# Layer 1's joined attention weights: eight of ten key chunks turned by the transposing DMA instead of four, with a new order of work

## The chip, the cores and the metric

One NeuronCore of one Trainium2 chip runs the whole program. The metric is device time in microseconds (us) of that core, median over runs. The kernel before takes 1679.44 us (three runs, 1678.99 to 1679.91).

## The reference, cut to what matters

Two layers over 1024 latent tokens and 256 context tokens, width 1024. Layer 0 is multi-head latent attention; the change leaves its instructions as they are. Layer 1 is differential attention with 8 heads: each head has two queries and two keys of 64 channels and one value of 128 channels.

```
scale = B_HEAD ** -0.5
o1 = attention(q[..., 0], k[..., 0], v)      # over 1024 latent keys + 256 context keys
o2 = attention(q[..., 1], k[..., 1], v)
o = o1 - lam_full * o2                        # the two maps share v
o = rms_norm(o, g_sub) * (1.0 - lambda_init)
o = o * silu(gate)
x = layer_norm(ALPHA * x + gate * (o @ out_w), ln_g, ln_b)
```

Since both maps multiply the same v, the kernel joins the two softmax maps into one weight matrix, p0 - lam * p1, before the product with v. Only the latent tokens are wanted after layer 1, so there are 8 heads x 8 tiles of 128 queries: 64 units, each over 1280 keys (10 chunks of 128).

## The kernel before

**One unit of layer 1** (`attend`, L1786 on). PE makes five PSUM banks of scores (L1845, L1846). DVE takes maxima (L1863 over the context, L1867 over the latent keys) and bounds (L1869); ACT takes exponentials into SBUF (L1874). DVE sums and joins: L1882 to L1884, then L1887, one instruction over 128x1280 in fp32, here called the **join**. The joined weights stand with queries on partitions; the product with v needs keys on partitions, so each 128x128 chunk has to be turned, and it is wanted in two float16 parts (high and low).

There are two ways to turn a chunk, and `KD` (L77) says how many chunks take which:

- *The PE way* (`turns`): PE transposes chunks KD to 9 in fp32 into PSUM (L1788; four chunks, then two), ACT writes the high part `ph` (L1793) and DVE the low part `pl` (L1795), both from PSUM.
- *The DMA way* (`far`): ACT writes the high part of chunks 0 to KD-1 into `dd` (L1892, **far.hi**), DVE the low part (L1893, **far.lo**), both from SBUF, and one transposing DMA on SP's queue turns both into `pd` (L1895, **far.move**). `dd` has one buffer, `pd` two.

`values` then makes 30 products of 128 columns into one PSUM bank (L1810 to L1812, **pv**), first those from `ph` and `pl`, then those from `pd`; ACT scales the result (L1816) and squares it (L1817), POOL normalises it and it goes to DRAM.

**What else PE does meanwhile.** While head h is attended, PE makes the keys, queries and values of head h+1 (`mm3`, L217 to L219); these fill the time in which a unit waits for other engines. During head 7 there is no next head; instead the output projection of finished tiles (`out_tile`, turns L1953, products L217 to L219 in fp32) fills it. It can begin only after the value buffers of the last head are let go: ACT's L1738 and POOL's L1739 split the values, ACT's L1741 makes the gate, SP stores it (L1742) and loads whole rows of it back (L1939), POOL multiplies (L1940), and PE turns (L1953).

**What sets the order.** `heads1` writes every piece of work of layer 1 with an engine, a cost and a due time into a list (`Plan.add`). `Plan.run` takes pieces from it by start time and, among those that could start within `EPS1` of the earliest on their engine, by due time; each kind's due time is moved by the table `OFF`, and nothing more than `AHEAD` ahead of the rest is taken. The resulting order is the program: every engine works through its own list in order, so a wait at its head holds all that stands behind. The table, `EPS1` and `AHEAD` are numbers written in the kernel; no part of the order is decided on the chip.

## Time and profile before

| | us |
|---|---|
| median of 3 runs | 1679.44 |
| profiled execution, its own time | 1678.12 |
| its span in the trace | 1676.3 |
| layer 0 and projections, up to the first unit | about 915 |
| heads 0 to 6 of layer 1, with the next head's projections | about 597 |
| head 7, with the output projection | about 164 |

A profile gives, for each engine, when it was busy. Each engine works in order, so an idle stretch ahead of an instruction means that it waited; the trace names the instruction whose end released it. A PE that is busy 98% of a stretch is what the stretch lasts by, and work of other engines there costs nothing until it makes PE wait. PE's matmuls overlap: the time that one occupies PE is the distance from its start to the next one's start, not its own duration.

### The profile page before, as it was taken

To read this page: it belongs to the slowest core of one execution; us is meant where nothing else is said; L and a number is where in the kernel's file an instruction comes from. 1 tells how busy PE (TensorE), PEld (TensorE's weight loads), DVE (VectorE), ACT (ScalarE), POOL (GpSimd) and SP (SyncE) were. 2 spreads that over 40 slices of the span, in tenths; PEclk is the share of its full clock that TensorE was granted. 3 is DMA by queue.
4 is the path that set the end of the run, shared out by engine and by line. 5 is a ranking of instruction groups with operands and counts; after the bars stand their busy time and mean duration, and the time that the engine had idled before them with its cause. 6 is when DMAs were issued, how large, how long until landed. Compare 5 with 4: busy or idle time off the path is not lost.

```text
span 1676.3 us, 36592 instructions
## 1 busy us (share of the span) xinstructions
...
## 2 busy tenths in 40 slices
...
GB/s 319 91 132 232 206 81 21 42 33 42 39 36 42 39 52 45 104 167 204 177 113 79 72 101 102 102 102 105 98 95 86 96 84 92 59 156 89 146 135 76
DMA packets 183932, 171.63 MB, mean 102 GB/s; under 512 B 82024, under 2 KB 159432, under 8 KB 183759
## 3 DMA queue, kind: packets, MB, share of 16 engines
...
## 4 chain that ended last, share of the span: by engine, by line
PE 65%; DVE 19%; ACT 9%; issue 3%; DMA 2%; POOL 2%; POOLq 0%; DVEq 0%; SPq 0%; ACTq 0%
PE ps_s L217 5%; PE ps_s L219 5%; PE ps_s L218 5%; PE ps_a L969 4%; PE ps_a L970 4%; PE ps_a L971 4%; PE ps_a L217 3%; PE ps_a L219 3%; PE ps_a L218 3%; ACT p L1874 3%; PE ps_a L920 3%; DVE mx L1867 3%; DVE p L1887 3%; PE ps_d L994 2%; PE ps_d L987 2%
## 5 line engine op out<-in xcount | busy, mean ns | idle before, releaser
L979 POOL TENSOR_TENSOR pl<-p,ph 128x1024 f16<-128x1024 f32 (+1 forms) x176 | 370.2, 2117 | 102.7 <-ACT ph L977 68.6
L975 ACT ACTIVATE p<-ps_a,esc 128x1024 f32<-128x1024 f32 (+1 forms) x176 | 188.7, 1072 | 58.9 <-PE ps_a L971 52.4
L924 DVE TENSOR_REDUCE mx<-ps_a 128x1 f32<-128x1024 f32 x128 | 156.2, 1222 | 72.1 <-PE ps_a L920 71.5
L1874 ACT ACTIVATE p<-ps_p,mx 128x512 f32<-128x512 f32 x256 | 175.5, 689 | 31.4 <-DVE mx L1869 30.6
L977 ACT CAST ph<-p 128x1024 f16<-128x1024 f32 (+1 forms) x176 | 177.0, 1006 | 7.0 <-PE ps_d L988 1.8
L1867 DVE TENSOR_REDUCE mx<-ps_p 128x1 f32<-128x512 f32 x256 | 164.2, 680 | 1.9 <-PE ps_p L1846 1.9
L969 PE MATMUL ps_a<-qH,KH 100*128 100x512 f16 x320 | 122.0, 381 | 3.1 <-DVE mx L924 2.3
L970 PE MATMUL ps_a<-qH,KL 96*128 96x512 f16 x320 | 121.5, 380 | 0.0
L971 PE MATMUL ps_a<-qL,KH 96*128 96x512 f16 x320 | 120.7, 377 | 0.0
L1795 DVE SCALAR_TENSOR_TENSOR pl<-ps_t,lcf,ph 128x512 f16<-128x512 f32 (+1 forms) x128 | 78.2, 611 | 42.5 <-ACT ph L1793 41.9
L1887 DVE SCALAR_TENSOR_TENSOR p<-p,sm,p 128x1280 f32<-128x1280 f32 x64 | 106.1, 1658 | 1.7
L1845 PE MATMUL ps_p<-KS,QS 128*128 128x512 f16 x256 | 98.1, 383 | 9.5 <-ACT p L1874 9.5
L987 PE MATMUL ps_d<-Vh,ph 128*128 128x65 f16 x1344 | 103.7, 194 | 2.0 <-ACT ph L977 1.7
L988 PE MATMUL ps_d<-Vl,ph 128*128 128x64 f16 x1344 | 103.2, 194 | 0.0
L1793 ACT ACTIVATE ph<-ps_t,lcf 128x512 f16<-128x512 f32 (+1 forms) x128 | 74.8, 584 | 39.3 <-PE ps_t L1788 38.1
L1846 PE MATMUL ps_p<-KS,Q 128*128 128x512 f16 x256 | 98.2, 383 | 0.0
L987 PEld LDWEIGHTS <-ph 128*128 128x128 f16 x1344 | 89.0, 98 | 11.2 <-issue 4.8
L988 PEld LDWEIGHTS <-ph 128*128 128x128 f16 x1344 | 87.3, 98 | 3.8
L191 POOL TENSOR_SCALAR ss<-ss 128x1 f32<-128x1 f32 x64 | 20.4, 318 | 119.1 <-ACT ps_t L1817 117.4
L920 PE MATMUL ps_a<-KH,qH 96*128 96x512 f16 x256 | 76.1, 379 | 0.0
L936 DVE TENSOR_REDUCE mx<-ps_a 128x4 f32<-128x1024 f32 (+1 forms) x48 | 50.3, 1048 | 33.9 <-PE ps_a L931 33.9
L1810 PE MATMUL ps_t<-vh,ph 128*128 128x128 f16 x384 | 68.4, 221 | 6.4 <-DVE pl L1795 6.3
...
## 6 DMA issues: line engine op xcount, KB each, us to landing
ws<-in_dw SPq DMA_DIRECT2D x28, 512.0 KB, 3.9
adw<-in_ada_w SPq DMA_DIRECT2D x24, 512.0 KB, 4.5
adaw<-in_ada_w SPq DMA_DIRECT2D x16, 512.0 KB, 6.8
g<-sg_d SPq DMA_DIRECT2D x16, 512.0 KB, 3.5
...
```

What stands on the lines that cost most here:

```text
L924: add("m.max", "D", 1.223, lambda t=t, ps=ps: dve.tensor_reduce(mx.tile[:, t, 0:1], ps.tile, axis=AX.X, op=ALU.max), r=[ps], w=[(mx, t)] i ...
L969: pe.matmul(s_, KH[i][:nr, ks], QH.tile[:nr, :], start=True, stop=False)
L970: pe.matmul(s_, KL[i][:DQ, ks], QH.tile[:DQ, :], start=False, stop=False)
L971: pe.matmul(s_, KH[i][:DQ, ks], QLo.tile[:DQ, :], start=False, stop=True)
L975: add("s.exp", "A", 1.114 if x else 0.682, lambda st=st, p32=p32: act.activation(p32.tile[:, :2 * n], st.tile[:, :2 * n], AF.Exp, scale=esc0),
L977: add("s.hi", "A", 1.046 if x else 0.618, lambda p32=p32, ph=ph: act.copy(ph.tile[:, :2 * n], p32.tile[:, :2 * n]), r=[p32], new=[ph], hol ...
L979: add("s.lo", "G", 2.14 if x else 1.17, lambda p32=p32, ph=ph, pl=pl: pool.tensor_tensor(pl.tile[:, :2 * n], p32.tile[:, :2 * n], ph.tile[ ...
L987: pe.matmul(v_()[:, t, :], w, Vh[:, k, h, :], start=(k == kcs[0] and t == 0), stop=False, skip_group_check=True)
L988: pe.matmul(v_()[:, t, :V0], w, Vl[:, k, h, :], start=False, stop=False, skip_group_check=True)
L1867: add(f"max{m}", "D", 0.68, lambda i=i, b_=b_: dve.tensor_reduce(mx.tile[:, 2 + 2 * m + i:3 + 2 * m + i], b_.tile, axis=AX.X, op=ALU.max, ...
L1874: add(f"exp{m}", "A", 0.78 if n == 512 else 0.57, lambda i=i, c0=c0, n=n, b=b, lo=lo: act.activation(p[m].tile[:, c0:c0 + n], b.tile[:, lo ...
L1887: add("join", "D", 1.65, lambda: dve.scalar_tensor_tensor(p[0].tile, p[1].tile, sm.tile[:, 4:5], p[0].tile, op0=ALU.mult, op1=ALU.add), r= ...
```

## The change

`KD` goes from 4 to 8. Per unit, PE turns two chunks (one group) where it turned six (two groups); far.hi and far.lo work on 1024 columns where they worked on 512; the transposing DMA turns 16 blocks of 128x128 (512 KB) where it turned 8 (256 KB). `pv` now starts with two chunks from `ph` and `pl` and takes eight from `pd`.

The buffers follow: `dd` and each `pd` double, `ph` and `pl` shrink to a third, `o1` goes from three buffers to two, a few constants of layer 0 (`onr`, `adac`, `cct`, `cols0`) move into a pool that closes with layer 0's first part, and `gb3` (the broadcast `ln_b`) moves to a pool that opens later, so its load now waits for `OPEN` rather than `PRJ`. The table `OFF`, `EPS1` and `AHEAD` are new, so layer 1's whole list is in another order.

```diff
-EPS1 = dict(P=0.05, A=0.05, D=0.2, G=0.2)
-AHEAD = 3.75
+EPS1 = dict(P=0.05, A=0.05, D=0.15, G=0)
+AHEAD = 3.5
-OFF = {"bound0": -5.35, "bound1": -0.75, "exp0": -1.25, "exp1": -2.1, "far.hi": -6.65, "far.lo": -2.1, "far.move":
+OFF = {"bound0": -7.75, "bound1": -2.7, "exp0": -0.85, "exp1": -2.0, "far.hi": -5.9, "far.lo": -1.95, "far.move":
...
-KD = 4
+KD = 8
...
-    onr = col(P, "onr", F32R)
-    adac = col(16, "adac")
-    cct = col(16, "cct")
+    p0 = ctx.enter_context(ExitStack())
+    early_ = p0.enter_context(spool("early"))
+    onr = early_.tile([P, P], F32R, name="onr")
+    adac = early_.tile([P, 16], F32, name="adac")
+    cct = early_.tile([P, 16], F32, name="cct")
...
-            "o1": ([P, P], F32, 3), "mx": ([P, 8], F32, 2), "sm": ([P, 8], F32, 4),
+            "o1": ([P, P], F32, 2), "mx": ([P, 8], F32, 2), "sm": ([P, 8], F32, 4),
...
-                for k0, n, a in ((0, 4, PR["t0"]), (4, 2, PR["t1"])):
+                for k0, n, a in ((0, 2, PR["t0"]),):
...
-                add("far.hi", "A", 0.72, lambda: act.activation(dd.tile[:, 0, :], p[0].tile[:, :KD * P], AF.Copy, scale=lcf[:, 0:1]), r=[p[0]], new=[dd], hold=0.63, at=g + PR["fa"])
+                add("far.hi", "A", 1.24, lambda: act.activation(dd.tile[:, 0, :], p[0].tile[:, :KD * P], AF.Copy, scale=lcf[:, 0:1]), r=[p[0]], new=[dd], hold=1.15, at=g + PR["fa"])
...
-            TAG1["g"] = ([P, D], F32, 2)
+            TAG1["g"], TAG1["gb3"], place["gb3"] = ([P, D], F32, 2), ([P, D], F32, 1), place["g"]
...
-                add("o.gb", "S", 4.0, lambda: bcast_row(GB[1].tile, ln_b[1:2, :]), r=[PRJ], new=[GB[1]], hold=0.06, at=g + 6.5)
...
+        add("o.gb", "S", 4.0, lambda: bcast_row(GB[1].tile, ln_b[1:2, :]), r=[OPEN], new=[GB[1]], hold=0.06, at=g)
```

(The planner's costs of far.lo and far.move change in the same way as far.hi's. Lines of the changed kernel stand one higher than before in layer 1: L1893 is L1894 there.)

Where the new order matters, three places. First, DVE's list in head 5, tile 4, from the join on. `mx` are the maxima, `dd` is far.lo, `pl` the PE way's low part, `wx` and `wy` the next head's weights. Before:

```order
L1863 TENSOR_REDUCE mx_20044<-ps_c_19994 128x2
L1867 TENSOR_REDUCE mx_20044<-ps_p_19937 128x1
L1867 TENSOR_REDUCE mx_20044<-ps_p_19952 128x1
L1869 TENSOR_SCALAR mx_20044<-mx_20044 128x1
L1893 SCALAR_TENSOR_TENSOR dd_20053<-p_3048_19919,lcf,dd_20053 128x512
L1867 TENSOR_REDUCE mx_20044<-ps_p_19969 128x1
L1867 TENSOR_REDUCE mx_20044<-ps_p_19988 128x1
L1869 TENSOR_SCALAR mx_20044<-mx_20044 128x1
L1795 SCALAR_TENSOR_TENSOR pl_20128<-ps_t_20091,lcf,ph_20100 128x512
L1613 SCALAR_TENSOR_TENSOR wx_20002<-ws_19513,uw_19800,wx_20002 128x1024
L1613 SCALAR_TENSOR_TENSOR wy_20022<-ws_19514,uw_19800,wy_20022 128x1024
L1795 SCALAR_TENSOR_TENSOR pl_20128<-ps_t_20145,lcf,ph_20100 128x256
```

The same place now:

```order
L1864 TENSOR_REDUCE mx_19710<-ps_c_19671 128x2
L1868 TENSOR_REDUCE mx_19710<-ps_p_19584 128x1
L1868 TENSOR_REDUCE mx_19710<-ps_p_19605 128x1
L1870 TENSOR_SCALAR mx_19710<-mx_19710 128x1
L1894 SCALAR_TENSOR_TENSOR dd_19715<-p_2994_19575,lcf,dd_19715 128x1024
L1868 TENSOR_REDUCE mx_19710<-ps_p_19682 128x1
L1868 TENSOR_REDUCE mx_19710<-ps_p_19687 128x1
L1870 TENSOR_SCALAR mx_19710<-mx_19710 128x1
L1796 SCALAR_TENSOR_TENSOR pl_19793<-ps_t_19707,lcf,ph_19729 128x256
L1614 SCALAR_TENSOR_TENSOR wx_19685<-ws_19347,uw_19611,wx_19685 128x1024
L1614 SCALAR_TENSOR_TENSOR wy_19739<-ws_19348,uw_19611,wy_19739 128x1024
```

far.lo stands where it stood, behind three maxima, but is twice as wide; of the two low parts of the PE way, the 512-wide one is gone.

Second, ACT's list at the end of head 6, where the last head's values are finished: L1738 (now L1739) splits the values, L1741 (now L1742) makes the gate, L1892 (now L1893) is far.hi. Before, from far.hi of head 6's last tile on; the gate (L1741) and the last two copies of values stand directly ahead of it:

```order
L1892 ACTIVATE dd_21813<-p_3321_21698,lcf 128x512
L1816 ACTIVATE o_3335_21817<-ps_t_21760,sm_21541 128x128
L1874 ACT_TABLE_LOAD
L1874 ACTIVATE p_3336_21820,sm_21821<-ps_p_21753,mx_21803 128x512
L1817 ACTIVATE ps_t_21760,ss_21824<-o_3335_21817 128x128
L1874 ACTIVATE p_3336_21820,sm_21821<-ps_p_21799,mx_21803 128x512
L1874 ACTIVATE p_3342_21841,sm_21821<-ps_p_21805,mx_21803 128x512
L1793 ACTIVATE ph_21846<-ps_t_21836,lcf 128x512
L1874 ACTIVATE p_3342_21841,sm_21821<-ps_p_21808,mx_21803 128x512
L1874 ACTIVATE p_3342_21841,sm_21821<-ps_c_21794,mx_21803 128x256
L1874 ACTIVATE p_3336_21820,sm_21821<-ps_c_21794,mx_21803 128x256
L1738 CAST vh_21863<-Vf_21301 128x1280
```

Now, up to far.hi of the same tile:

```order
L1736 COPY gg_20822<-ps_s_21176 128x256
L1734 ACTIVATE Vf_20875<-ps_s_21176,kc_95 128x256
L1875 ACTIVATE p_3264_21324,sm_21290<-ps_p_21248,mx_21256 128x512
L1739 CAST vh_21333<-Vf_20875 128x1280
L1875 ACTIVATE p_3264_21324,sm_21290<-ps_p_21253,mx_21256 128x512
L1875 ACTIVATE p_3264_21324,sm_21290<-ps_c_21228,mx_21256 128x256
L1817 ACTIVATE o_3270_21369<-ps_t_21326,sm_20975 128x128
L1742 ACT_TABLE_LOAD
L1742 ACTIVATE gg_20822<-gg_20822,uw_20212 128x1024
L1818 ACTIVATE ps_t_21326,ss_21388<-o_3270_21369 128x128
L1893 ACTIVATE dd_21391<-p_3257_21289,lcf 128x1024
```

The split of the values stood behind far.hi of head 6's last tile and a whole unit's exponentials; it now stands one exponential behind the last copy of values, ahead of that far.hi.

Third, SP's queue at the same place. `pd<-dd` is far.move; the first of each listing is that of head 6's tile 7 (before) and tile 6 (now). `sg_d<-gg` stores the gate, `g<-sg_d` loads it back, `wsq` and `gb` are the broadcast rows. Before:

```order
L1895 DMA_TRANSPOSE pd_21826<-dd_21813 128x8x128
L1831 DMA o_d_100<-o_3335_21817 128x128
L1895 DMA_TRANSPOSE pd_21925<-dd_21879 128x8x128
L1742 DMA sg_d_98<-gg_21274 128x8x128
L1165 DMA wsq_21965<-in_ln_g 128x1024
L1939 DMA g_21967<-sg_d_98 128x1024
L1831 DMA o_d_100<-o_3355_21918 128x128
L1939 DMA g_21994<-sg_d_98 128x1024
L1895 DMA_TRANSPOSE pd_22054<-dd_22031 128x8x128
```

Now:

```order
L1896 DMA_TRANSPOSE pd_21307<-dd_21261 128x16x128
L1939 DMA ws_21312<-o_d_103 128x896
L1939 DMA ws_21380<-o_d_103 128x896
L1743 DMA sg_d_101<-gg_20822 128x8x128
L1939 DMA ws_21401<-o_d_103 128x896
L1940 DMA g_21421<-sg_d_101 128x1024
L1166 DMA gb_3285_21423<-in_ln_b 128x1024
L1166 DMA wsq_21425<-in_ln_g 128x1024
L1832 DMA o_d_103<-o_3270_21369 128x128
L1896 DMA_TRANSPOSE pd_21431<-dd_21391 128x16x128
```

The gate's store and its first load stood behind far.move of head 7's first tile; they now stand ahead of far.move of head 6's last tile, two transposing DMAs earlier. In PE's list the scores of about 2.3 units stand between the last product of the values and the first turn of the output projection before, and of about 1.4 units now. In the steady part a unit's pv stood behind the second to fifth score bank of the unit two on; now it mostly stands behind the first or second bank of the unit three on.

## Rows read from the trace of the kernel before

**Rows 1.** Busy us and instructions of each engine by stretch; granted clock, DMA share, GB/s.

```profile
1005.00:1512.00 507.00, 497.40 (x4302) 365.63 (x4300) 456.52 (x839) 411.45 (x1065) 251.21 (x308) 1.00 0.41 98
1512.00:1541.70 29.70, 17.14 (x137) 11.42 (x134) 23.99 (x36) 25.14 (x54) 13.60 (x13) 0.83 0.37 94
...
1556.00:1676.30 120.30, 112.31 (x702) 88.51 (x700) 82.05 (x144) 50.76 (x126) 67.06 (x62) 0.98 0.37 115
```

**Rows 2.** DVE's waits, 1005 to 1512 us: us in total, times, longest.

```profile
DVE pl L1795 <- ACT ph L1793: 28.1, 27, 1.7
```

**Rows 3.** PE in order of time, one group of four turns: start, us, instruction.

```profile
1207.07 0.60 PE L1788 MATMUL ps_t<-idr,p 128*128 128x128 f32 x4
...
1207.51 0.38 PE L217 MATMUL ps_s<-h1H,wy 128*128 128x512 f16 x1
```

**Rows 4.** Groups by shape, 915 to 1655 us: busy us, mean ns | idle before.

```profile
L1893 DVE SCALAR_TENSOR_TENSOR dd<-p,lcf,dd 128x512 f16<-128x512 f32 x64 | 58.1, 907 | 1.5 <-ACT dd L1892 1.3 <-issue 0.2
...
L1795 DVE SCALAR_TENSOR_TENSOR pl<-ps_t,lcf,ph 128x512 f16<-128x512 f32 x64 | 47.5, 743 | 26.0 <-ACT ph L1793 26.0
L1892 ACT ACTIVATE dd<-p,lcf 128x512 f16<-128x512 f32 x64 | 46.0, 718 | 27.0 <-DVE p L1887 20.1 <-issue 5.2 <-ACT kH L1679 0.7
...
L1793 ACT ACTIVATE ph<-ps_t,lcf 128x512 f16<-128x512 f32 x64 | 43.9, 686 | 22.6 <-PE ps_t L1788 22.5
...
L1793 ACT ACTIVATE ph<-ps_t,lcf 128x256 f16<-128x256 f32 x64 | 30.9, 483 | 16.7 <-PE ps_t L1788 15.6
L1795 DVE SCALAR_TENSOR_TENSOR pl<-ps_t,lcf,ph 128x256 f16<-128x256 f32 x63 | 30.2, 480 | 16.5 <-ACT ph L1793 15.9
...
L1613 DVE SCALAR_TENSOR_TENSOR wx<-ws,uw,wx 128x1024 f16<-128x1024 f32 x13 | 21.1, 1620 | 0.0
...
L1611 ACT ACTIVATE wx<-ws,uw 128x1024 f16<-128x1024 f32 x13 | 15.1, 1158 | 0.3
```

**Rows 5.** Two lines of DVE: ns min/median/max, first and last start.

```profile
L1795 DVE SCALAR_TENSOR_TENSOR pl<-ps_t,lcf,ph x128: 470/609/752, 931.8 to 1655.2; 128x512 f16<-128x512 f32 x64, 128x256 f16<-128x256 f32 x64
...
L1893 DVE SCALAR_TENSOR_TENSOR dd<-p,lcf,dd x64: 740/743/2918, 929.0 to 1649.4; 128x512 f16<-128x512 f32 x64
```

**Rows 6.** far.move, ns min/median/max and landing; the page's plain 512 KB load (us).

```profile
L1895 SPq DMA_TRANSPOSE pd<-dd x64: 1232/1244/2240, 929.8 to 1651.5; - x64
...
DMA to landing us min/median/max: 3.0/3.1/4.4
...
g<-sg_d SPq DMA_DIRECT2D x16, 512.0 KB, 3.5
```

**Rows 7.** One unit in order of time, DVE, ACT, SP and PE: start, us.

```profile
1202.96 2.41 DVE L1887 SCALAR_TENSOR_TENSOR p<-p,sm,p 128x1280 f32<-128x1280 f32 x1
...
1205.41 0.72 ACT L1892 ACTIVATE dd<-p,lcf 128x512 f16<-128x512 f32 x1 [0.71 <-DVE p L1887]
...
1207.39 0.74 DVE L1893 SCALAR_TENSOR_TENSOR dd<-p,lcf,dd 128x512 f16<-128x512 f32 x1
...
1208.20 1.25 SPq L1895 DMA_TRANSPOSE pd<-dd  x1
...
1213.66 1.56 DVE L1887 SCALAR_TENSOR_TENSOR p<-p,sm,p 128x1280 f32<-128x1280 f32 x1
...
1215.17 0.22 PE L1810 MATMUL ps_t<-vh,pd 128*128 128x128 f16 x1
1215.23 0.22 PE L1811 MATMUL ps_t<-vl,pd 128*128 128x128 f16 x1
```

**Rows 8.** From the last values to the first turn of the output projection, in time.

```profile
1521.45 1.29 ACT L1738 CAST vh<-Vf 128x1280 f16<-128x1280 f32 x1
...
1530.59 0.57 SPq L1742 DMA_DIRECT2D sg_d<-gg  x1
...
1534.48 0.32 SPq L1939 DMA_DIRECT2D g<-sg_d  x1
...
1541.75 0.66 PE L1953 MATMUL ps_t<-idr,ws 128*128 128x128 f32 x4 [1.82 <-POOL ws L1940]
```

More of the change, by code (lines that the diff above doesn't have):

```diff
@@ L43 @@
 PR = dict(s0=0.0, mx=0.1, ex=0.2, t0=0.15, t1=0.4, s1=0.3, pv=0.7, jo=0.6, fa=0.75)
-EPS1 = dict(P=0.05, A=0.05, D=0.2, G=0.2)
-AHEAD = 3.75
+EPS1 = dict(P=0.05, A=0.05, D=0.15, G=0)
+AHEAD = 3.5
 SP0, SP1, SP2 = 0.0, 0.3, 3.3
-OFF = {"bound0": -5.35, "bound1": -0.75, "exp0": -1.25, "exp1": -2.1, "far.hi": -6.65, "far.lo": -2.1, "far.move":
-       3.05, "g.add": 0.6, "g.bias": 2.4, "g.keep": -1.25, "g.load": 0.25, "g.sum": -0.9, "g.zero": 0.35, "join":
-       -0.35, "k.ctx": -2.6, "k.hi": 0.4, "k.lo": -4.1, "k.move": 2.95, "late": -2.2, "max.c": -0.1, "max0": -7.45,
-       "max1": 0.15, "o.ga": -3.35, "o.gb": 2.0, "o.hi": 2.4, "o.lo": -1.9, "o.load": -3.1, "o.mul": -1.8, "open":
-       -1.65, "prod": 0.2, "pv": -4.6, "pv.gate": -0.65, "pv.norm": 1.1, "pv.out": -1.2, "pv.sq": -5.9, "pv.store":
-       -6.45, "pv.us": 1.9, "q.hi": 2.05, "q.lo": 1.5, "q.move": -5.7, "r.add": -2.6, "r.cos": 1.3, "r.out": 0.1,
-       "r.sin": -7.3, "r.swap": -0.15, "score0": 0.45, "score1": 0.35, "scorec": -0.05, "sums": -3.95, "turn.hi0":
-       -3.05, "turn.hi4": -5.7, "turn.lo0": 1.05, "turn.lo4": -3.25, "turn0": -0.3, "turn4": -2.6, "v.gate": -1.6,
-       "v.hi": 1.15, "v.keep": 1.5, "v.lo": -2.05, "v.octx": -1.7, "v.out": 2.55, "v.pctx": 0.05, "v.silu": 0.95,
-       "v.store": 4.4, "v.turn": -2.5, "w.hi": -0.85, "w.lo": 0.4, "w.load": -2.65, "w.root": -3.8, "w.scale": 2.3,
-       "w.sq": 1.4, "w.sum": -3.5, "w.unit": 0.6, "w.us": -0.25, "x.gate": 1.05, "x.hi": -0.65, "x.lo": 1.15,
-       "x.load": 3.15, "x.low": 4.3, "x.mul": 5.75, "z.add": -0.9, "z.agg": 0.15, "z.bn": 0.6, "z.end": 2.7, "z.g":
[3 rows of a table removed]
@@ new lines @@
+OFF = {"bound0": -7.75, "bound1": -2.7, "exp0": -0.85, "exp1": -2.0, "far.hi": -5.9, "far.lo": -1.95, "far.move":
+       2.25, "g.add": 0.05, "g.bias": 2.25, "g.keep": -1.65, "g.load": 0.2, "g.sum": -2.2, "g.zero": -1.5, "join":
+       -0.5, "k.ctx": -1.35, "k.hi": 2.7, "k.lo": 0.55, "k.move": 3.6, "late": -2.55, "max.c": -0.1, "max0": -11.6,
+       "max1": -0.4, "o.ga": 3.35, "o.gb": 3.1, "o.hi": 2.25, "o.lo": 0.85, "o.load": -3.7, "o.mul": -0.7, "open":
+       -5.4, "prod": 0.6, "pv": -6.15, "pv.gate": -0.5, "pv.norm": 0.9, "pv.out": -3.4, "pv.sq": -9.9, "pv.store":
+       -7.3, "pv.us": 1.8, "q.hi": 2.6, "q.lo": 0.15, "q.move": -7.6, "r.add": -3.25, "r.cos": 2.05, "r.out": -1.9,
+       "r.sin": -5.6, "r.swap": 1.65, "score0": 0.45, "score1": 0.35, "scorec": -0.45, "sums": -5.05, "turn.hi0":
+       -0.9, "turn.hi4": -5.7, "turn.lo0": 2.55, "turn.lo4": -3.25, "turn0": -1.95, "turn4": -2.6, "v.gate": -1.0,
+       "v.hi": -3.15, "v.keep": 2.45, "v.lo": -5.2, "v.octx": 1.7, "v.out": 2.35, "v.pctx": -0.4, "v.silu": -1.05,
+       "v.store": -0.15, "v.turn": -1.85, "w.hi": 1.9, "w.lo": 1.25, "w.load": -0.5, "w.root": -0.8, "w.scale": 2.1,
+       "w.sq": 1.45, "w.sum": -1.2, "w.unit": 0.05, "w.us": -2.6, "x.gate": -1.0, "x.hi": -3.15, "x.lo": 2.15,
+       "x.load": -3.65, "x.low": 2.4, "x.mul": 5.15, "z.add": -3.85, "z.agg": 0.95, "z.bn": 0.6, "z.end": -2.65,
[3 rows of a table added]
@@ L161, in hybrid_kernel @@
     gsub = col(1, "gsub")
-    cols0 = cpool.tile([P, 16, 2], F32, tag="cols0", name="cols0")
+    cols0 = early_.tile([P, 16, 2], F32, name="cols0")
     cols1 = cpool.tile([P, 16, 2], F32, tag="cols1", name="cols1")
@@ L197, in hybrid_kernel @@
     latL = lat.tile([P, 3, NTOK], F32R, name="latL")
-    p0 = ctx.enter_context(ExitStack())
     hp = p0.enter_context(spool("p0"))
```

10 lines of the change are left out of this document (5 added, 5 removed), and 6 rows, old and new, of the table OFF.

## The prediction, made before the changed kernel ran

> **What bounds the kernel now.** I read the windows first. From 1005 to 1512 us (heads 1 to 6) PE is busy 497.4 of 507.0 us at a granted clock of 1.00, DVE 456.5, ACT 411.5 [rows 1]: the reader is to see that this stretch lasts as long as PE's list, with DVE close behind. Head 7 from 1556 us on is also PE's, 112.3 of 120.3. Between them lies a gap, 1512 to 1541.7, where PE has 17.1 us of work in 29.7 us and its granted clock falls to 0.83 on average, between the levels of 1.2 and 2.4 GHz [rows 1]. Then I read the waits of DVE, since it is next: of its 50.5 idle us in the long stretch, 28.1 are waits of the PE way's low part for ACT's high part [rows 2]. Last I followed one unit through DVE, ACT, SP's queue and PE [rows 7] and the gap through its links [rows 8].
>
> The sum is made against the profiled execution's own 1678.1 us (span 1676.3); that is 1.3 us under the median of the three runs, 1679.4, so 1.3 is added at the end.
>
> **PE's turns.** A group of four turns holds PE from 1207.07 to the next matmul's start at 1207.51, 0.44 us [rows 3] (the 0.60 shown includes the tail that the next one overlaps). This group goes, once in each of 64 units: 64 x 0.44 = 28.2 us of PE. pv keeps its 30 products; nothing is added on PE. Where PE is the bound all of it is gained, so the upper bound is 28.2 (1.3 of it in the three units of the gap, where PE waits anyhow; I leave it in); the lower one depends on DVE and on the DMA, next.
>
> **ACT.** Removed per unit: a 512-wide copy from PSUM (0.686) and the 512-wide far.hi (0.718) [rows 4]. Added: a 1024-wide far.hi, by the row of the same shape, L1611, 1.158. Net -0.25 us; ACT had 95 us to spare in 507, so this is worth nothing by itself.
>
> **DVE.** Removed: the 512-wide low part, 0.743, and the 512-wide far.lo, 0.907 in the mean [rows 4]. Added: a 1024-wide far.lo. Twice the step from 256 to 512 columns (0.743 - 0.480 = 0.263) on top of 0.743 gives 1.27 for it undisturbed; the wide row L1613 on `wx` has a mean of 1.62 [rows 4]. I take 1.27 plus the 0.16 by which far.lo's mean now stands over its median of 0.743 [rows 5], so 1.43. DVE saves 1.65 - 1.43 = 0.22 us per unit, bounds 0.03 and 0.38. Rows 1 hold 48 units: DVE's work falls from 456.5 to 446, PE's time from 507 to 507 - 48 x 0.44 = 485.9. That leaves DVE 40 us of idle time where it had 50.5. It has to lose 10.5 us of waiting, and a source is there: a unit had two waits of the low part, and has one now, behind two maxima and a bound in DVE's list. If half of the 28.1 us goes, 36 us of idle time are left, under the 40. So PE stays the bound, with 4 us to spare in 486. I count the whole 28.2.
>
> Which form of DVE work is left matters here. far.lo reads both operands from SBUF and ran up to 2918 ns where its median is 743; the low part of the PE way reads one from PSUM and never passed 752 in 128 instructions [rows 5]. The Trainium skill, "SBUF — State Buffer", section "Who interferes with whom", says that a DVE instruction with two SBUF inputs contends with a GpSimd instruction that reads SBUF, and that whichever starts first holds the other off; the trace agrees, with those two maxima. It speaks against this change, which moves DVE work from the form that is never held off to the one that is: by it far.lo's mean would be nearer the 1.62 of L1613, DVE's work in the long stretch 9 us more, its idle time 31 us where I want 36, and the gain there some 5 us less.
>
> By rows alone that end is the 0.03, and it is kept in the first rival.
>
> **The transposing DMA.** far.move takes 1.244 us on SP's queue and lands 3.1 us after its issue [rows 6]. Twice the blocks: between 4.35 (only the issue part doubles) and 6.2 us (all of it doubles); less than 3.1 is excluded, since nothing of the transfer is left out. I take 4.35: the nearest row of that size, a plain 512 KB load, lands in 3.5 [rows 6], by that end. Who waits for it is pv. In the unit of rows 7 the DMA is issued at 1208.20 and its result is first used at 1215.17, 6.97 us later, so 3.9 us are to spare. Used up: 0.53 by the longer far.lo (far.hi, 0.44 longer, still ends ahead of it), 1.25 to 3.1 by the DMA, and 0.7 because pv reaches `pd` after two chunks where it did after six (12 products, 0.06 us from start to start [rows 7]). That is 2.5 to 4.3 of 3.9; PE's new list puts pv about half a unit later against the scores, some 5 of the 10.7 us that a unit takes there [rows 7], which gives back more than is missing. Cost taken: nothing. SP's queue has room, and what stands behind far.move (stores of a unit's output) nobody waits for at once.
>
> **The gap.** Its links before: the last values split at 1521.45, the gate stored at 1530.6, loaded back from 1534.5, first turn at 1541.75 [rows 8]. The store stood behind two far.moves and the split behind an exponential group, not behind missing data. The new lists put the split about one unit and the store two far.moves earlier, and PE has scores of 1.4 units there for 2.3. PE's idle time in the gap is 29.7 - 17.1 = 12.6 us over three units [rows 1], 4.2 each: one unit fewer saves 4.2. Bounds: all 12.6, or one unit more, +4.2.
>
> **Costed at nothing.** The constants that move: layer 0's lists are the same, and the new pool closes where the old buffers' last readers are long done. `o1`'s third buffer: hidden by ACT's idle time, 95 us over 48 units [rows 1], some 2 us each; without that cover pv's output would wait for a store of about as long. `gb3`'s load is later by the opening of its pool, hidden by the first output tile, whose end is its first reader; uncovered it costs one 512 KB load, 3.5 [rows 6].
>
> **Sum.** 1678.1 - 28.2 - 4.2 = 1645.7 in the profiled execution; with 1.3, a median of 1647.0. Its own range: the gap's bounds (-8.4, +8.4) and PE's 9.6 us of remaining idle time in the long stretch, some of which may go: 1634 to 1657.
>
> **Rivals.** *DVE takes over.* PE's turns go, but DVE's waits are replaced by others as its list tightens, and idle time stays at 50.5. For it: DVE is busy 90% now and would be 92%; far.lo, now twice as long, stands ahead of two maxima that free score banks. Against it: half of DVE's idle time is tied to what is removed. Then a unit shortens by DVE's 0.22 alone: 64 x 0.22 = 14, gap unchanged: 1664, median 1665; with DVE's saving at its lower bound (0.03), 1676 to 1677.
>
> *pv waits for the DMA (the change doesn't do what it says).* If landing is 6.2 or more and the later place of pv is worth little, each unit waits 0.4 to 0.6 us and gives back the 0.44: 1675 to 1688. For it: the spare 3.9 above; against it: the unit is pipelined deeper.
>
> *The single `dd` buffer (slower).* far.hi of a unit must wait until the DMA of the unit before has read `dd`. The loop is far.hi to issue (1205.41 to 1208.20, 2.79 [rows 7]; 3.3 with the wider far.lo) plus landing: 7.7 to 9.5 us against a unit of 10.70 (1202.96 to 1213.66 [rows 7]). It decides once landing passes 7.4 us; at 8 us each of 56 units outside head 7 costs 0.6 more than before: +34 us, 1712. For it: one buffer, and other DMAs fill 0.41 of the engines' time; against it: the longest landing now is 4.4 [rows 6].
>
> **How the numbers follow.** Forecast 0.72; DVE takes over 0.18; pv waits 0.06; the `dd` loop 0.04. The likeliest is 1647. A range for 8 in 10 reaches from 1634 to 1668: the forecast's own, and the middle of DVE's case. A measurement of this kernel can tell 0.2%, 3.4 us, from no change. Faster: the forecast, DVE's case but for 0.01, and 0.02 of pv's, together 0.91; same: that 0.01 and 0.02 of pv's, 0.03; slower: the last 0.02 of pv's and the `dd` loop, 0.06.
>
> **What would show it.** Right: 128 turns in place of 384 and a far.move that lands in 4.3 to 5 us; heads 1 to 6 shorter by 3.5 us each at a PE busy share still near 98%; DVE's waits for ACT's high part halved; the first turn of the output projection 20 to 25 us after the last values. Wrong: a PE busy share of 95% or less in heads 1 to 6, with waits of pv for `pd` (the second rival), for maxima or joins (the first), or of ACT ahead of far.hi for a DMA (the third); or a gap as long as before.

## The result, and the profile after

The changed kernel takes 1683.25 us in the median of 16 runs (1679.68 to 1688.34), the kernel before 1679.39 in the same job: a ratio of 1.0025, with a 95% interval of 1.0017 to 1.0033. The forecast was 1647.0, with a range of 1634 to 1668; it was wrong in sign and by 36 us. The profiled execution has a span of 1682.0 us for 1676.3.

PE's turns did go: its busy time over the whole span falls from 1610.6 to 1590.1 us. The time did not follow. These are the windows of the changed kernel, in the columns of [rows 1]:

```profile
1005.00:1512.00 507.00, 479.86 (x4101) 343.79 (x4099) 453.78 (x787) 407.02 (x1012) 279.36 (x309) 1.00 0.52 118
1512.00:1541.70 29.70, 16.06 (x137) 12.16 (x135) 24.61 (x30) 22.57 (x49) 21.38 (x18) 0.83 0.71 196
1556.00:1682.00 126.00, 113.02 (x710) 88.10 (x708) 84.67 (x147) 52.77 (x134) 69.05 (x65) 0.99 0.48 131
```

In the long stretch PE's share falls from 98.1 to 94.6%: it now waits inside it. DVE does about as much as before, 453.8 us for 456.5 [rows 1]. A fixed window holds different amounts of work in the two kernels, so the same five heads are set side by side: from the join of head 1's first unit to that of head 6's. (The join of head 7's first unit would be a bad end: it stands 1 us behind the split of the last values before, and 20 us behind it now, so that the window would take in the gap in one kernel alone.) The first line is before, the second after.

```profile
1009.70:1437.90 428.20, 419.65 (x3629) 308.28 (x3628) 388.24 (x713) 352.37 (x905) 205.77 (x257) 1.00 0.40 95
```

```profile
1013.50:1444.70 431.20, 407.25 (x3479) 291.64 (x3478) 387.67 (x676) 351.27 (x869) 232.46 (x259) 1.00 0.52 118
```

Five heads last 3.0 us longer. PE is busy for 12.4 us less. DVE is busy for as long as before, and its idle time grows from 40.0 to 43.5 us. By the forecast's own terms the five heads were to last 428.2 - 40 x 0.44 = 410.6, with DVE busy for 388.2 - 40 x 0.22 = 379.4 and idle for 31.2. So of the 20.6 us that are missing here, 8.3 are DVE's work and 12.3 its waiting. Of the rest of the program, what lies ahead of these heads takes 3.8 us longer, and what lies behind them 1.1 us less.

The work. These groups of DVE, by shape, are from 1005 to 1512 us; first before, then after (busy us, mean ns, idle before it):

```profile
L1887 DVE SCALAR_TENSOR_TENSOR p<-p,sm,p 128x1280 f32<-128x1280 f32 x47 | 77.7, 1652 | 1.2
L1893 DVE SCALAR_TENSOR_TENSOR dd<-p,lcf,dd 128x512 f16<-128x512 f32 x47 | 36.1, 768 | 0.2 <-issue 0.2
L1795 DVE SCALAR_TENSOR_TENSOR pl<-ps_t,lcf,ph 128x512 f16<-128x512 f32 x48 | 35.6, 742 | 12.8 <-ACT ph L1793 12.8
...
L1884 DVE SCALAR_TENSOR_TENSOR sm<-sm,nlam 128x1 f32<-128x1 f32 x48 | 20.0, 416 | 1.7
L1613 DVE SCALAR_TENSOR_TENSOR wx<-ws,uw,wx 128x1024 f16<-128x1024 f32 x11 | 18.5, 1683 | 0.0
L1636 DVE TENSOR_TENSOR rr<-rr,cosB 128x512 f32<-128x512 f32 x12 | 16.3, 1358 | 0.0
...
L1636 DVE TENSOR_TENSOR kr<-kr,cosB 128x512 f32<-128x512 f32 x12 | 8.2, 681 | 0.0
```

```profile
L1888 DVE SCALAR_TENSOR_TENSOR p<-p,sm,p 128x1280 f32<-128x1280 f32 x47 | 74.0, 1575 | 1.7
L1894 DVE SCALAR_TENSOR_TENSOR dd<-p,lcf,dd 128x1024 f16<-128x1024 f32 x48 | 65.7, 1368 | 2.9 <-ACT dd L1893 2.9
...
L1885 DVE SCALAR_TENSOR_TENSOR sm<-sm,nlam 128x1 f32<-128x1 f32 x47 | 28.8, 613 | 1.7
...
L1637 DVE TENSOR_TENSOR kr<-kr,cosB 128x512 f32<-128x512 f32 x12 | 14.7, 1226 | 0.2
...
L1614 DVE SCALAR_TENSOR_TENSOR wx<-ws,uw,wx 128x1024 f16<-128x1024 f32 x11 | 14.0, 1271 | 0.0
...
L1637 DVE TENSOR_TENSOR rr<-rr,cosB 128x512 f32<-128x512 f32 x12 | 8.3, 691 | 0.4
```

The wide low part costs 1.37 us, a little under the 1.43 taken. But the narrow one that it replaces costs 0.768 in this stretch, not the 0.907 of the whole layer [rows 4]; so by durations DVE saves 0.742 + 0.768 - 1.368 = 0.14 per unit. The saving is less still, since DVE's instructions overlap as PE's do: in the timeline below the join starts at 1239.20, takes 1.56, and the next instruction starts at 1240.68, 0.08 us before its end. Two instructions made into one lose one such overlap, which leaves 0.06 per unit.

The third step of the sums, on one column, grows from 416 to 613 ns, 9.5 us over 48 units. Other DVE instructions change by as much the other way: the join by -3.6 us, the rope's cosine steps by -8.0 (`rr`) and +6.5 (`kr`), `wx` by -4.5. So in this stretch the new list makes DVE lose no more time in such instructions in all; the time lies elsewhere, on a step that stands between the exponentials and the join. The timeline shows how the step is held (start, us). GpSimd starts a wide operation 0.14 us ahead of it, and the step lasts until that ends:

```profile
1236.54 0.15 DVE L1883 TENSOR_REDUCE sm<-sm 128x2 f32<-128x6 f32 x1
1236.73 0.17 DVE L1884 RECIPROCAL sm<-sm 128x2 f32<-128x2 f32 x1
1236.93 2.24 DVE L1885 SCALAR_TENSOR_TENSOR sm<-sm,nlam 128x1 f32<-128x1 f32 x1
1239.20 1.56 DVE L1888 SCALAR_TENSOR_TENSOR p<-p,sm,p 128x1280 f32<-128x1280 f32 x1
1240.68 0.68 DVE L1864 TENSOR_REDUCE mx<-ps_c 128x2 f32<-128x512 f32 x1
...
1236.79 2.36 POOL L1767 TENSOR_TENSOR oL<-ws,oH 128x1024 fp32r<-128x1024 f32 x1 [3.44 <-ACT oH L1766]
```

Of its 64 instances 30 are over 300 ns (mean 1066), 21 of them beside GpSimd's rope add (L1639); before, 16 were (mean 867), 7 beside the rope add. The others take 222 to 223 in the mean. That is 25.3 us of holding, for 10.3. The new list places the rope's cosine step just ahead of the sums in 16 of 64 units (2 before), and the add follows it on GpSimd.

The waiting. DVE's and PE's waits after, 1005 to 1512 us (in total, times, longest):

```profile
DVE sm L1883 <- ACT p L1875: 32.0, 24, 2.8
DVE rsw L1636 <- ACT kr L1634: 6.1, 5, 1.4
DVE dd L1894 <- ACT dd L1893: 2.9, 6, 0.6
...
PE ps_p L1846 <- ACT p L1875: 13.0, 14, 1.8
PE ps_t L1811 <- DVE pl L1796: 10.2, 9, 1.8
```

The 28.1 us of [rows 2] are gone to the last tenth. In their place DVE waits 32.0 us for the exponentials in front of the sums (3.6 before): a low part of the PE way stood directly ahead of the sums in 35 of 64 units, and does in 12 now. PE waits for score banks, which the exponentials free, and for the low part.

The transposing DMA, as in [rows 6]:

```profile
L1896 SPq DMA_TRANSPOSE pd<-dd x64: 1545/1912/5366, 931.7 to 1657.6; - x64
...
DMA to landing us min/median/max: 4.2/4.5/6.2
```

Its landing is close to the 4.35 that was taken. Its hold on SP's queue is 1.9 us and up to 5.4, for 1.24 and 2.24.

The gap and what follows it. From the split of the last values to the first turn of the output projection, and from there to the end; first before, then after:

```profile
1521.45:1541.75 20.30, 10.15 (x85) 7.34 (x84) 17.43 (x25) 15.75 (x34) 12.18 (x9) 0.81 0.46 120
```

```profile
1541.75:1676.30 134.55, 124.67 (x760) 97.78 (x760) 93.19 (x160) 56.81 (x142) 77.48 (x69) 0.99 0.39 117
```

```profile
1514.80:1536.83 22.03, 12.17 (x106) 9.49 (x104) 17.61 (x20) 17.71 (x38) 15.56 (x12) 0.77 0.84 228
```

```profile
1536.83:1682.00 145.17, 128.34 (x779) 99.44 (x777) 99.31 (x170) 64.14 (x157) 78.15 (x73) 0.98 0.46 125
```

PE's idle time in the gap is 9.9 us for 10.2, and behind it 16.8 for 9.9.

### The profile page after: what moved, and what is told of

Read it like the earlier page. It is cut to its first block, busy times and chain, and to the rows that moved or that the text cites. A ratio compares the mean times of both kernels' runs of the same rounds, so it can differ in the third digit from the quotient of the medians.

```text
span 1682.0 us, 35977 instructions
## 1 busy us (share of the span) xinstructions
PE 1590.1 (95%) x14052; PEld 1179.5 (70%) x14052; DVE 1263.0 (75%) x1941; ACT 1136.9 (68%) x2164; POOL 943.6 (56%) x772
## 5 line engine op out<-in xcount | busy, mean ns | idle before, releaser
L1893 ACT ACTIVATE dd<-p,lcf 128x1024 f16<-128x1024 f32 x64 | 73.3, 1146 | 37.5 <-DVE p L1888 33.4
L193 POOL TENSOR_SCALAR ss<-ss 128x1 f32<-128x1 f32 x64 | 34.2, 534 | 105.4 <-ACT ps_t L1818 102.5
L1811 PE MATMUL ps_t<-vh,pd 128*128 128x128 f16 x512 | 91.1, 222 | 0.0
L1812 PE MATMUL ps_t<-vl,pd 128*128 128x128 f16 x512 | 91.0, 221 | 0.0
L1813 PE MATMUL ps_t<-vh,pd 128*128 128x128 f16 x512 | 90.9, 221 | 0.0
L1894 DVE SCALAR_TENSOR_TENSOR dd<-p,lcf,dd 128x1024 f16<-128x1024 f32 x64 | 86.9, 1358 | 3.4 <-ACT dd L1893 3.3
```

## Experiments

All differences below are against the changed kernel, from the two ratios to the kernel before (0.001 is 1.68 us; each interval reaches 1.3 to 2.4 us to either side, so that a difference of 2 us or less is not told from none).

**The order alone and the buffers alone.** `e1` has the old numbers in the changed kernel; `e4` is the kernel before with the rest of the diff's buffers:

```diff
 # e1, in after
-EPS1 = dict(P=0.05, A=0.05, D=0.15, G=0)
-AHEAD = 3.5
+EPS1 = dict(P=0.05, A=0.05, D=0.2, G=0.2)
+AHEAD = 3.75
 # and OFF as before
 # e4, in before
-"o1": ([P, P], F32, 3)
+"o1": ([P, P], F32, 2)
 # and the pool "early", and gb3 in the pool a1outg
```

> The changed kernel (eight chunks by DMA, buffers moved) with the numbers of before for the order of layer 1's list (offsets, tolerances, look-ahead). Order theory (eight chunks by DMA gain, and the new order loses it again): with the old numbers the 28 us of PE's turns show up, 1650 to 1665. DVE theory (DVE is the bound with eight chunks, whatever the order): 1680 to 1690, as the changed kernel. Third theory, the one I hold likeliest: the old numbers were chosen for other durations, so the list they now make is looser, with PE waiting for exponentials and values more often: slower than the changed kernel, 1690 to 1725; then the new order is a part of what keeps the change near even and not its cost.

Measured 1716.3, ratio 1.0217 (1.0203 to 1.0231): 32 us slower. The third theory held. There PE waits 15.0 us for `pd` and 11.6 for score banks. With the old numbers eight chunks cost 32 us more, so the new list belongs to the change.

> The kernel before with only the buffers moved as in the change (constants in a pool that closes, two output buffers in place of three, the second output row of constants loaded later); four chunks by DMA and the old numbers. All theories but one: same as before within 3 us, 1677 to 1682. Buffer theory (the two output buffers delay pv's output, or the late load the output tiles): slower by 4 us or more.

Measured 1680.37, ratio 0.9997 (0.9989 to 1.0006): nothing, as forecast.

**The held step.** `e2`, and the same edit in the kernel before (`e5`):

```diff
-dve.scalar_tensor_tensor(s_[:, 4:5], s_[:, 3:4], nlam, s_[:, 0:1], op0=ALU.mult, op1=ALU.mult)
+dve.tensor_scalar(s_[:, 4:5], s_[:, 3:4], nlam, s_[:, 0:1], op0=ALU.mult, op1=ALU.mult)
```

> The changed kernel with one instruction of DVE in another form: the third step of the sums (lambda times a quotient, one column) as a tensor-scalar operation, with the two other factors as scalars, in place of one with two tensors in SBUF; the list is the same. In the trace of the changed kernel this step has a mean of 613 ns, and of its 64 it is over 300 ns in 30, with a mean of 1066 ns, each beside a GpSimd operation on two SBUF tensors (27 beside the rope add or the output weights); undisturbed it is 223 ns; before it was over 300 ns in 16 of 64. Hold-off theory (this step stands between the exponentials and the join, on the path that everything else waits for): the step falls to 270 ns, as the bound's tensor-scalar step (273 ns), with no long ones, and 30 times 0.8 us less some of it that was waited out anyway, 12 to 20 us, go: 1663 to 1671. Order theory and queue theory (what costs is the place of the exponentials in the lists, or SP's queue): the held step was filled with waiting anyway, under 4 us: 1679 to 1683.

Measured 1671.65, ratio 0.9948 (0.9934 to 0.9961): 13 us faster than the changed kernel and faster than before. The lines of both steps in `e2` (ns, min/median/max):

```profile
L1885 DVE TENSOR_SCALAR sm<-sm,nlam x64: 272/273/275, 923.8 to 1637.2; 128x1 f32<-128x1 f32 x64
...
L1888 DVE SCALAR_TENSOR_TENSOR p<-p,sm,p x64: 1544/1553/3266, 924.1 to 1637.5; 128x1280 f32<-128x1280 f32 x64
```

The step is never held in this form. The join behind it, still on two tensors, is held instead: a mean of 1828 ns from 1005 to 1512 us, for 1575 in the changed kernel. The Trainium skill, "SBUF — State Buffer", section "Who interferes with whom", says this of the two forms: a DVE instruction with at most one SBUF input, outside the 2-port perf modes, doesn't contend with GpSimd, and one with two does when the GpSimd instruction reads SBUF. The trace agrees, 64 times of 64 for the first.

> The kernel before with the third step of the sums in the tensor-scalar form, nothing else. There the step was over 300 ns in 16 of 64, with a mean of 867 ns, 10.3 us above its undisturbed 222 ns; in the changed kernel it was 25.3 us (30 of 64, 1066 ns), and the same edit took 11.6 us there, because the join right behind it was then held in its place (mean 1828 ns for 1575). Hold-off theory: the edit is worth 40% of the 10.3 here too, 3 to 6 us: 1674 to 1677, so that what the new list adds by hold-offs is the difference, some 7 us. Rival (the form gains for another reason, equal in both): 1668 to 1670.

Measured 1676.79, ratio 0.9988 (0.9978 to 0.9999): 2 us under the kernel before, less than even the hold-off theory's 3 to 6. So most of the held step's price came with the change. Whether that is because the new list holds it more (25.3 us for 10.3), or because PE was the bound before, isn't told apart.

`e10` takes the other side away:

```diff
-pool.tensor_tensor(r.tile[:, c], r.tile[:, c], sw.tile[:, :n], op=ALU.add)
+pool.tensor_tensor(r.tile[:, c][:, :1], r.tile[:, c][:, :1], sw.tile[:, :1], op=ALU.add)
```

> The changed kernel with GpSimd's rope add made for one column of 512, so that keys and queries lack the rotated part; it takes the place of the 1.27 us add in GpSimd's list, and all lists are the same. Hold-off theory: the add is what holds the sums' third step (22 of the 30 long ones stand beside it); with it gone, that step is long in about 8 of 64, and the join isn't held in its place: 12 to 18 us go, 1665 to 1671. Rival (the held step was only one of many waits, as good as any other): under 5 us, above 1678.

Measured 1669.38, ratio 0.9940 (0.9928 to 0.9953): 14 us, as the hold-off theory said. The median of the step is 219 ns, 10 of 64 are still held, and the join isn't held more (over 1700 ns in 4 of 64, for 5).

`e8` cuts the add in two pieces, on top of `e2`:

```diff
-pool.tensor_tensor(r.tile[:, c], r.tile[:, c], sw.tile[:, :n], op=ALU.add)
+for u in (slice(0, n // 2), slice(n // 2, n)):
+    pool.tensor_tensor(r.tile[:, c][:, u], r.tile[:, c][:, u], sw.tile[:, u], op=ALU.add)
```

> The changed kernel with the sums' third step in the tensor-scalar form (1671.65) and, on top, GpSimd's rope add in two pieces of half the width. In the trace of that kernel the join is over 1700 ns in 29 of 64, 20 of them beside this add (7.2 us in all). Hold-off theory: a piece of half the length holds the join half as long, 2 to 4 us go: 1667 to 1670. Rival (the join then waits for both pieces, or GpSimd's longer list makes keys and queries late): 1671 to 1675.

Measured 1678.96, ratio 1.0001 (0.9992 to 1.0010): 9 us slower than `e2`, and beyond even the rival's 1671 to 1675. The pieces of keys and queries cost 1079 and 772 ns in the mean where the whole took 1353 and 1271, and ACT waits 11.2 us for the keys' add, for 1.1 in `e2`: the rival's second reason.

**What bounds.** `e6` halves the low part, `e11` does the two turns three times:

```diff
 # e6, far.lo with n = 512
+pool.memset(dd.tile[:, 1, n:], 0.0)
-dve.scalar_tensor_tensor(dd.tile[:, 1, :], p[0].tile[:, :KD * P], lcf[:, 0:1], dd.tile[:, 0, :], ...)
+dve.scalar_tensor_tensor(dd.tile[:, 1, :n], p[0].tile[:, :n], lcf[:, 0:1], dd.tile[:, 0, :n], ...)
 # e11, in the turns
-for j in range(n):
+for j in (*range(n),) * 3:
```

> The changed kernel, with the low part of the DMA way's chunks made for 512 of 1024 columns only and zero for the others (written by GpSimd), so that four of ten chunks lack their low part; the list is the same. It takes about 0.6 us of DVE per unit, 39 us over 64 units. DVE theory (DVE's list, with its held steps, is what the units now last): 15 to 30 us go, 1653 to 1668. PE theory (PE's work is still the bound): at most 5. Wait theory (what costs is DVE waiting for the exponentials behind the second bound, 32 us of it in heads 1 to 6): DVE waits that much longer there, under 10 us go, 1674 to 1683.

Measured 1664.65, ratio 0.9920 (0.9906 to 0.9933): 18 us. The instruction's mean falls from 1368 to 832 ns, 34 us over 64 units; half of that comes back as time. The five heads show where the other half went, as DVE's idle time, 52.9 us for 43.5:

```profile
1009.70:1429.70 420.00, 406.52 (x3481) 291.79 (x3479) 367.09 (x676) 349.50 (x869) 231.07 (x299) 1.00 0.54 122
```

Of `e2`'s edit, by contrast, nothing was lost: DVE's busy time from 915 us on falls by 12.5 us there (651.1 to 638.6), and the kernel is 13 faster.

> The changed kernel with each pair of TensorE turns done three times over into the same place, so that TensorE has again six turns per unit, as before the change (4 x 0.11 us more per unit, 28.2 us over 64), while DVE, ACT and the DMAs do what they do in the changed kernel. If TensorE were still the bound, as the prediction had it: 20 to 28 us more, 1703 to 1711. DVE theory: most of it falls into TensorE's waits, 0 to 10 us more, 1683 to 1693.

Measured 1690.05, ratio 1.0070 (1.0058 to 1.0083): 8 of 28.2 us. In these two runs PE's work is worth a quarter of its length, DVE's low part a half. That is the prediction's main step turned round.

**DMA and SP's queue.** `e3` moves rows of the finished list, `e7` moves the high part alone:

```diff
 # e3, after the list is made, for each w.load
+back = the k.move and q.move among the 30 steps ahead of it, unless a step between reads them
+they go right behind the w.load
 # e7
-sp.dma_start_transpose(pd.tile.rearrange("p a k q -> p (a k) q"), dd.tile.rearrange("p a c -> p (a c)"))
+sp.dma_start_transpose(pd.tile[:, 0], dd.tile[:, 0])
-(pd.tile[:, 0, kc, :], pd.tile[:, 1, kc, :])
+(pd.tile[:, 0, kc, :], pd.tile[:, 0, kc, :])
```

> The changed kernel with one thing altered in SP's queue: the two loads of the next weights are issued ahead of the four to eight moves of keys or queries that stand just before them. The lists of the other engines are the same. In the trace of the changed kernel the loads of one chain leave at 1291.84, behind a transposing DMA of 1.84 us and four moves of 2.4 us, and ACT, whose squares of them stand ahead of exponentials, waits 9.0 us for them in heads 1 to 6 (before: none). Queue theory (SP's longer queue is a cause): ACT's waits for the weights go and the time falls by 3 to 8 us, to 1675 to 1680. Hold-off theory: at most 2 us.

Measured 1683.72, ratio 1.0020 (1.0011 to 1.0029): nothing, although ACT's wait for the weights fell from 9.0 us to this:

```profile
ACT wsq L1583 <- DMA ws<-in_dw: 0.9, 3, 0.4
```

> The changed kernel, with the transposing DMA for the high part alone (eight blocks as before the change, not sixteen), and the value products taking the high part a second time in place of the low one, so that the low part of eight chunks is left out; DVE still makes it, and all lists are the same but for that. Packets per unit fall back to those of before, SP's issue from 1.85 to about 1.25 us, the landing from 4.4 to 3.1 us, and the plain loads' landing from 4.9 to 3.9. DMA theory (traffic, landing or SP's queue cost): 6 us or more go, under 1677. DVE theory: no more than 3 us, 1680 to 1684.

Measured 1680.1, ratio 1.0007 (0.9998 to 1.0016): 3 us, with about 2 of noise. All that the wider DMA costs in traffic, landing and queue is about that.

**The order of DVE's list.** `e9` moves one step of the finished list, here in one unit; `e16` adds `e2`'s form.

```diff
 L1870 TENSOR_SCALAR mx<-mx 128x1
-L1894 SCALAR_TENSOR_TENSOR dd<-p,lcf,dd 128x1024
 L1868 TENSOR_REDUCE mx<-ps_p 128x1
 L1868 TENSOR_REDUCE mx<-ps_p 128x1
 L1870 TENSOR_SCALAR mx<-mx 128x1
+L1894 SCALAR_TENSOR_TENSOR dd<-p,lcf,dd 128x1024
```

> The changed kernel with one instruction moved in DVE's list: in 53 of 64 units the low part of the DMA way stands behind the second pair of maxima and its bound, where it stood between the two pairs; its transposing DMA leaves that much later, and nothing else in the lists moves. In the changed kernel DVE waits 32.0 us in heads 1 to 6 for the exponentials that follow the second bound, and PE 13.0 us for score banks that the exponentials free. Wait theory (the order of DVE's list, maxima late, costs): the second bound comes 1.3 us earlier, the exponentials too, and the low part fills the wait: 4 to 10 us go, 1673 to 1679. DVE theory in its strict form (DVE has no time left, whatever its order): at most 2 us, 1681 to 1685.

Measured 1681.18, ratio 1.0015 (1.0006 to 1.0024): 2 us, not clear of noise and under the wait theory's bounds. DVE's wait for the exponentials fell to 24.6 us, but the transposing DMA leaves later, and ACT's far.hi now waits for the one `dd` buffer, 17.2 us where it was 2.3:

```profile
ACT dd L1893 <- DMA pd<-dd: 17.2, 11, 2.3
```

So one wait was traded for another, and what the order of DVE's list alone is worth isn't shown.

> The changed kernel and its list with two small edits that had a result alone: the sums' third step in the tensor-scalar form (1671.65) and the low part of the DMA way behind the second bound in 53 units (1681.18, 2 us under the changed kernel). If they add up, 1668 to 1671; if the earlier exponentials bring the sums closer to GpSimd's rope add, so that the join is held more often, 1672 to 1676.

Measured 1674.74, ratio 0.9975 (0.9966 to 0.9984): 4 to 5 us slower than `e2`. They don't add up. The rival's time came true, but hardly for its reason: the join is over 1700 ns in 31 of 64, for 29 in `e2`. The wait for `dd` is there again, 17.1 us.

**Less work with both, and a list made anew.** `e13` is `e2` and `e6` together. `e12`, `e14` and `e15` replace the list's numbers and, ahead of it, the steps' durations:

```diff
+seen = {"far.move": (1.85, 4.6), "k.move": (2.5, 5.0), "q.move": (4.8, 7.2), "w.load": (1.1, 5.6), "pv.store": (0.33, 2.4)}
+more = {"far.lo": 0.12, "sums": 0.05, "r.cos": 0.13}   # and 0.2 for every step of GpSimd
 # e15: "far.move": (2.2, 6.5)
 order = pl_.run(EPS1, AHEAD)
```

> The changed kernel and its list, with both the sums' third step in the tensor-scalar form (alone: 1671.65) and the low part of the DMA way made for 512 of 1024 columns only, the rest zero (alone: 1664.65); so DVE has about 0.9 us less per unit. DVE theory: the two add up, 1652 to 1656, and PE is the bound again only there. Loop theory (the round DVE to ACT to DVE of one unit is the bound once DVE is lighter): less than half of the second gain is left, 1660 to 1666.

Measured 1659.02, ratio 0.9885 (0.9871 to 0.9898): 11 us under `e2`, so 60% of the second gain is left, between the two theories. With DVE busy for 363.7 us in the five heads, for 387.7 in the changed kernel, they last 415.4, still over the forecast's 410.6, and 1647 is 12 us away.

> The changed kernel with the sums' third step in the tensor-scalar form, and layer 1's list made anew once more: the list is drawn up with the durations that the trace of the changed kernel shows where the source had others (SP holds 1.85 us per transposing DMA and 2.5 per group of four key moves where it counted 0.06 and 0.24, weights 5.6 us until they land where it counted 4.0, the low part 0.12 us longer, the rope's cosine step 0.13, GpSimd's steps 0.2), and with offsets sought for these. In every unit DVE now has both pairs of maxima and bounds first, then the low part, then the weights' or rope's step, and then the sums; the cosine step stands apart from its swap. Work is the same. List theory (the work fits, and the waiting comes from the order and the times it was made with): the exponentials' wait is filled, heads 1 to 6 are PE's again, 20 to 30 us under 1671.65: 1640 to 1655. DVE theory in its strict form (DVE's work and its round through ACT are the bound in any order): 1665 to 1673. Third: a list made from mean durations loses it again to held steps, above 1673.

Measured 1681.63, ratio 1.0016 (1.0007 to 1.0025): 11 us slower than `e2`, in the range of the third case, but not for its reason: DVE is busy for less than in `e2`, 375.3 us in the five heads for 385.0. Its waits, 1005 to 1512 us:

```profile
PE ps_t L1813 <- DMA pd<-dd: 20.1, 7, 4.9
...
ACT dd L1895 <- DMA pd<-dd: 25.4, 10, 4.1
```

With the low part last in the unit the transposing DMA leaves late, and both of my DMA rivals came up there, `pv` and the one `dd` buffer. The five heads of `e2` and of `e12`, and one stretch of `e12`:

```profile
1009.60:1437.70 428.10, 406.87 (x3480) 291.64 (x3478) 385.04 (x676) 351.50 (x870) 236.20 (x259) 1.00 0.53 119
```

```profile
1097.80:1104.60 6.80, 4.10 (x28) 3.15 (x29) 1.67 (x3) 4.53 (x13) 0.00 (x0) 0.50 0.68 159
1006.00:1446.90 440.90, 417.27 (x3488) 298.92 (x3486) 375.29 (x676) 346.77 (x868) 254.79 (x260) 0.97 0.53 120
```

Of the 12.8 us that `e12` is longer here, 10.4 are PE's busy time, for the same work, and 2.4 its idle time. Its granted clock is at 1.2 GHz in six stretches of heads 1 to 6, 27 us in all (in `e2` in none), each at a wait of PE of 2.2 to 4.9 us, five of the six for `pd`. Five of these stretches, 24 us, lie in the five heads; at half the clock they are up to 12 us of PE's work (an estimate from these figures). So most of what this list lost here came by the clock that fell at its waits.

> As e12_list_as_timed, but with the sums' third step in the form of the changed kernel, on two tensors in SBUF. If the new list keeps GpSimd's wide operations away from the sums, it is the same as e12 within 3 us; if they still meet, it is 6 to 12 us slower. The difference to 1683.25 is what the list alone gives.

Measured 1692.94, ratio 1.0086 (1.0072 to 1.0100): 12 us slower than `e12`; the two still meet in that list, where the step is over 300 ns in 27 of 64, 23 of them beside the rope's sine step on GpSimd. By itself the list is 10 us slower than that of the changed kernel.

> As e12_list_as_timed (1681.63), with one duration changed for which its list was drawn up, and new offsets sought: the transposing DMA counts 2.2 us on SP and 6.5 until it lands, where e12 counted 1.85 and 4.6. In e12's trace TensorE waits 20.1 us for the transposed weights in heads 1 to 6 and ACT's high part 25.4 us for the one buffer that the DMA still reads, and SP is held up to 5.7 us by one such DMA; both waits are at most 2.3 us in the changed kernel. DMA theory (e12 lost by its late transposing DMAs, and the list theory holds otherwise): these waits fall under 8 us each and the time under 1665. DVE theory (in any order the round DVE to ACT to DVE is full): 1668 to 1680. Third: other waits of a list made from means take their place, above 1680.

Measured 1662.46, ratio 0.9904 (0.9890 to 0.9917): 20 us under the changed kernel, 7 under `e2`, and the fastest that leaves nothing out; 16 us faster than before. The DMA theory's time held. No wait of PE for `pd` is left; ACT's for `dd` fell from 25.4 to 9.4 us, not under the 8 that the theory asked for. These are some of its waits, 1005 to 1512 us, and then its window of the five heads from join to join:

```profile
ACT dd L1895 <- DMA pd<-dd: 9.4, 6, 3.0
...
DVE sm L1885 <- ACT p L1877: 23.1, 14, 3.8
...
PE ps_t L1813 <- DVE pl L1798: 10.8, 10, 3.7
```

```profile
1008.70:1428.10 419.40, 406.83 (x3471) 291.09 (x3469) 379.65 (x676) 346.69 (x863) 228.06 (x257) 1.00 0.54 121
```

That is 11.8 us less than in the changed kernel for the same work: 8.0 of them are DVE's busy time, 3.8 its idle time. DVE is now busy for the forecast's 379.4 us, and idle for 39.8, as before the change (40.0).

## Why the prediction was wrong, step by step

- *PE's turns, 28.2 us.* The work went as said: 128 turns, and PE's busy time in five heads falls by 12.4 us of 17.6 (probably since a matmul with a wait behind it shows its whole tail as busy, as the 0.60 in [rows 3]). That all of it is gained was wrong. `e11` gives it back to PE and costs 8 us.
- *"DVE saves 1.65 - 1.43 = 0.22 us per unit."* This is the first step that failed. The stretch had 0.14 by durations, because the mean of the removed instruction was taken over the whole layer, where a few held ones raise it, and about 0.06 by distances from start to start, which the prediction used for PE and not for DVE. In the five heads DVE saved 0.6 us in all, where 8.8 were forecast. And the sums' third step is held more often, a cost outside the edited lines that the new order made; no term of the sum held it. In heads 1 to 6 it adds nothing to DVE's total, since other instructions got shorter by as much, but where it stands it counts: taking it away is worth 13 us (`e2`), taking away GpSimd's add 14 (`e10`).
- *"If half of the 28.1 us goes, 36 us of idle time are left, under the 40. So PE stays the bound."* This is the second, and it is the step on which the sign hung. The wait of the low part went wholly, and as much came up in front of the sums: in the five heads DVE is idle for 43.5 us, where 31.2 were forecast. Idle time was taken for a sum of separate waits, of which one can be struck out. Two runs speak against that: in `e6` DVE has 20.6 us less to do in the five heads and is idle for 9.4 more, and in `e3` its wait for the exponentials falls from 32.0 to 23.9 us and ACT's for the weights from 9.0 to 0.9, but DVE is busy for 5.3 us more in the five heads, and nothing is gained. The likeliest reading, argued from the waits and not shown by a run of its own, is that idle time is what is left of a round, maxima to bound to exponentials to sums to join, that DVE and ACT go through one after the other; a shorter piece of DVE's work between two of these leaves a longer wait at the next.
- *The rule of the Trainium skill.* It was weighed against the low part, which was the wrong instruction: its mean is 1368 ns, 0.09 us above its median of 1276. What the rule struck is the small step, where GpSimd's add now stands, and in `e2` the join behind it.
- *The transposing DMA, cost nothing.* Nearly right: landing 4.5 for 4.35, no wait of `pv`, and 3 us in all (`e7`). That SP has room was right in effect only (`e3`); its hold is up to 5.4 us. The margin is small: with the low part later in the unit the one `dd` buffer costs ACT 17 us of waiting (`e9`, `e16`).
- *The gap, -4.2.* Wrong. The values were split at 1514.80 and the first turn of the output projection came at 1536.83, 22.0 us later for 20.3 [rows 8], although the scores of about one unit fewer stand between; PE's idle time there is 9.9 us for 10.2, so it doesn't go by the number of units. The sign that the prediction named, 20 to 25 us from split to turn, came true and told nothing, since it was 20.3 before. Behind the gap PE is idle for 7 us more than before, for which the sum had no term.
- *Costed at nothing: constants, `o1`, `gb3`.* Right (`e4`).

Of the rivals, *DVE takes over* named what happened, with its condition (idle time stays, it was 50.5 and is 53.2) and its end of 1676 to 1677; it was given 0.18. It missed the last 6 us: it let DVE's work shrink by a little and its idle time stay, where the work stayed and the idle time grew. Its middle, 1665, is near `e15` (1662), where DVE's busy time is the forecast's and its idle time that of before; but `e15` has the sums' other form, which the rival didn't have, so that the nearness is in part luck. The other two hardly showed in the changed kernel (ACT waits 2.3 us for `dd`) and did in `e12`, the last also in `e9` and `e16`.

What stays open: the best version has 15 us more than the forecast. Its five heads last 419.4 for 410.6, and nearly all of that is DVE's idle time, 39.8 for 31.2. Whether another order fills more of it wasn't settled. Nor was a new list tried with four chunks by DMA, so that how much of `e15`'s gain needs eight is open too.
